# Hybrid decoder trunk on one core: the last output projection reads half of its weights already split, and the two row blocks are finished one after the other

## The chip, the cores and the metric

The kernel runs on 1 core of one Trainium2 chip. The metric is the device time of one execution in microseconds (us). Before the change the median of three runs is 2597.0 us (2596.93 to 2600.05). Engines are named as in the profile: PE is TensorE (matmul), PEld its weight load, DVE is VectorE, ACT is ScalarE, POOL is GpSimd, SP is SyncE, which here only issues DMA transfers. ACT and POOL also have a DMA queue each.

## The reference

Four layers; layer i has mixer i mod 3, so the last one (i = 3) is again multi-head latent attention. Everything is float32, with 256 rows of 2048.

```python
def reference(x, mem, norm_in, final_norm, mem_norm, rel_bias, w_in_a, ...):
    mem_n = _rmsnorm(mem, mem_norm)
    for i in range(DEPTH):
        h = _rmsnorm(x, norm_in[i])
        ...
            self_out, mq, gate = _mla_branch(h, w_in_a[j], ...)
        ...
        mem_out = _memory_attention(mq, mem_n @ w_mem_kv[i])
        y = jnp.concatenate([self_out, mem_out], axis=-1) * jax.nn.silu(gate)
        x = x + y @ w_out[i]
    return _rmsnorm(x, final_norm)

def _rmsnorm(x, g):
    xf = x.astype(jnp.float32)
    y = xf * lax.rsqrt(jnp.mean(xf * xf, axis=-1, keepdims=True) + EPS)
    return (y * g.astype(jnp.float32)).astype(x.dtype)
```

`y` has 3072 columns (2048 of the mixer, 1024 of the memory heads), so `w_out[i]` is 3072 x 2048. What the change touches is the last 512 rows of `w_out[3]`, the last residual addition, the final norm and the output.

## The kernel before

The 256 rows stand as two blocks `t` of 128 partitions; the running sum is `x[0]`, `x[1]` (128 x 2048 each, in SBUF for the whole run). A float32 product is made of three matmuls of float32r parts: each operand is split into a high part (`copy_act`, an ACT copy to float32r, line 60) and a low part (DVE subtraction, line 69), and the product is high x high + high x low + low x high.

Weights stream in through `stage` (line 205): one transfer on SP's queue of 512 KB, two blocks of 128 weight rows by 512 columns, into one of five `wr` buffers. `parts_of` (line 233) splits one block of 128 x 512 into `wh` and `wl` (three buffers each). `rows_by` (line 239) goes over the weight blocks `k` and multiplies each by both row blocks `t`: three matmuls of 512 columns for each `k` and `t` (lines 264 to 266), into two PSUM accumulators of the tag `acc` (four buffers). `columns_by` (line 269) is the same for products that come out transposed; the gates use it with the layer's normed input `nm.at`, four tiles of the tag `xT`.

The mixer's output comes in six parts `y` of 512 columns, in the order 4, 0, 1, 2, 3, 5 (line 984). Behind each part follows `w_out` (line 963) of the part before it: for each of four blocks `c` of 512 output columns a `rows_by` over the part's four weight blocks, then one addition into `x` for each row block (line 968). So the last call, `w_out` of part 5, stands alone at the end of the program.

In this last call each `c` is also squared and summed (line 978, ACT, into `f4`) and multiplied by the final norm's weights `fg` into `xg` (line 979, DVE). When all four are done, the sums of both row blocks are reduced, `rsqrt_mean` (line 151) works out the scale factors of both blocks with 12 small DVE instructions, and lines 1010 to 1018 scale and write four pieces of 128 x 1024: those of rows 0 to 127 by DVE and SP's queue, those of rows 128 to 255 by ACT and ACT's queue.

The order of instructions on each engine is worked out when the program is built, from dependences, buffers and assumed durations; an instruction may stand ahead of one that is written earlier. `tc.keep_in_program_order` ties an instruction behind the one written before it on its engine, and `tc.issue_after(i)` ties those of a block behind `i`; both set the order only. Side work is written as a generator in the list `steps`: `other_work` (line 228) advances the first one by two turns at each weight stage, which sets where its instructions are written.

`part_tile` gives one of two buffers of 128 x 512 (tag `hl`); only the grouped mixers of layers 1 and 2 use them. The tags `big0`, `big1` and `big2` hold the latent mixer's compressed vectors until its last projection, and then `xg` and `fg`.

Of the kernel before, what the change touches and what calls it, by code (L numbers as in the profile page):

```python
# [8 lines left out]
F32 = mybir.dt.float32  # L9
F32R = mybir.dt.float32r  # L10
I32 = mybir.dt.int32
AF = mybir.ActivationFunctionType
OP = mybir.AluOpType
AX = mybir.AxisListType

P = 128
S = 256
D = 2048
EPS = 1e-6
# [12 lines left out]
def kernel(ctx: ExitStack, tc: tile.TileContext, a: dict, out: bass.AP,  # L32
                             kinds=(0, 1, 2, 0)):
    nc = tc.nc
    depth = len(kinds)
    cst = ctx.enter_context(tc.tile_pool(name="cst", bufs=1))
    wp = ctx.enter_context(tc.tile_pool(name="wp", bufs=1))
    act = ctx.enter_context(tc.tile_pool(name="act", bufs=1))
    wk = ctx.enter_context(tc.tile_pool(name="wk", bufs=1))
    ps = ctx.enter_context(tc.tile_pool(name="ps", bufs=1, space=bass.MemoryType.PSUM))  # L40
    dr = ctx.enter_context(tc.tile_pool(name="dr", bufs=1, space=bass.MemoryType.DRAM))
# [4 lines left out]
    def tmp(name, n=512, dt=F32):  # L46
        return wk.tile([P, n], dt, name=name, tag=f"t{n}", bufs=3)

    def small(name, n, dt=F32, bufs=None):
        return wk.tile([P, n], dt, name=name, tag=f"s{n}" if bufs is None else name,  # L50
                       bufs=bufs or 6)

    def f32(ap):
        return ap.bitcast(F32)

    def part_tile(dt=F32R):
        return wk.tile([P, 512], dt, name="hl", tag="hl", bufs=2)

    def copy_act(o, i, scale=1.0):
        inst = nc.scalar.activation(o, i, AF.Copy, scale=scale)  # L60
        if pinned:
            tc.keep_in_program_order(inst)
# [9 lines left out]
    x = [cst.tile([P, D], F32, name=f"x{t}") for t in range(2)]  # L72
# [73 lines left out]
    def not_before(col):  # L146

        tc.keep_in_program_order(nc.gpsimd.tensor_copy(small("tick", 1), col))


    def rsqrt_mean(dst, ssq, n):
        m = ssq.shape[-1]
        v = small("rv", m)
        nc.vector.tensor_scalar(v, ssq, 1.0 / n, EPS, op0=OP.mult, op1=OP.add)
        i0 = small("ri", m, I32)
        nc.vector.tensor_scalar(i0, v.bitcast(I32), 1, None, op0=OP.arith_shift_right)
        i1 = small("rj", m, I32)
        nc.vector.tensor_scalar(i1, i0, -1.0, float(0x5F3759DF), op0=OP.mult, op1=OP.add)
        y = i1.bitcast(F32)
        for it in range(3):  # L160
            u = small("ru", m)
            nc.vector.scalar_tensor_tensor(u, y, -0.5, y, op0=OP.mult, op1=OP.mult)
            w = small("rw", m)
            nc.vector.tensor_mul(w, u, v)
            y2 = dst if it == 2 else small("ry", m)
            nc.vector.scalar_tensor_tensor(y2, w, 1.5, y, op0=OP.add, op1=OP.mult)
            y = y2
# [31 lines left out]

    def square_sum(col, src):  # L200
        junk = tmp("junk")
        nc.scalar.activation(junk[:, :src.shape[-1]], src, AF.Square, accum_out=col)


    def stage(w, k0, m, cols, each=None):
# [20 lines left out]
    steps = []  # L226

    def other_work():
        for _ in range(2):
            if steps and next(steps[0], None) is None:  # L230
                steps.pop(0)

    def parts_of(wr, c0, n):
        wh = wp.tile([P, 512], F32R, name="wh", tag="wh", bufs=3)
        wl = wp.tile([P, 512], F32R, name="wl", tag="wl", bufs=3)
        split(wh[:, :n], wl[:, :n], wr[:, c0:c0 + n])
        return wh, wl

    def rows_by(xt, kts, w, k0, cols, name, prepare=None, each=None, late=None):


        acc = [ps.tile([P, 512], F32, name=f"acc_{name}{t}", tag="acc", bufs=4) for t in range(2)]
        for s in range(0, kts, ST):
            m = min(ST, kts - s)
            wr, n = stage(w, k0 + s, m, cols, each)
            other_work()
            for k in range(m):
                if prepare is not None:
                    prepare(s + k)
                wh, wl = parts_of(wr, k * n, n)  # L250
                q = xt[(s + k) // 4]
                for t in range(2):
                    xh, xl = (q[:, v, (s + k) % 4, t * P:(t + 1) * P] for v in range(2))
                    first, last = s + k == 0, s + k == kts - 1
                    if late is not None and t == 0:

                        both = late[:, s + k].rearrange("p v c -> p (v c)")
                        if not last:
                            nc.tensor.matmul(acc[t][:, :n], both, wh[:, :n], start=first, stop=False)
                        nc.tensor.matmul(acc[t][:64, :n], both[:, :64], wl[:, :n], start=False, stop=False)  # L260
                        if last:
                            nc.tensor.matmul(acc[t][:, :n], both, wh[:, :n], start=False, stop=True)
                        continue
                    nc.tensor.matmul(acc[t][:, :n], xh, wh[:, :n], start=first, stop=False)  # L264
                    nc.tensor.matmul(acc[t][:, :n], xh, wl[:, :n], start=False, stop=False)  # L265
                    nc.tensor.matmul(acc[t][:, :n], xl, wh[:, :n], start=False, stop=last)  # L266
        return acc
# [682 lines left out]
            return y  # L950


    nm = Norm(0)
    memory()
    copies = [(v, g) for v in range(2) for g in range(4)]

    for i in range(depth):
        kind = kinds[i]
        mixer = Latent(nm, i, kinds[:i].count(0)) if kind == 0 else Grouped(nm, i, kind == 1)
        mixer.first()  # L960
        nxt = Norm(i + 1) if i + 1 < depth else None

        def w_out(part, y, last):
            for c in range(4):
                acc = rows_by([y], 4, a["w_out"][i], part * 4, (c * 512, 512), "wo")
                for t in range(2):
                    xs = x[t][:, c * 512:(c + 1) * 512]
                    nc.vector.tensor_add(xs, xs, acc[t])  # L968
                if c == 0 and copies:

                    not_before(xs[:, :1])
                    table_copies(*copies.pop(0))
                if last and nxt is not None:
                    nxt.chunk(c)
                if last and nxt is None:
                    for t in range(2):
                        xs = x[t][:, c * 512:(c + 1) * 512]
                        square_sum(f4[:, t * 4 + c:t * 4 + c + 1], xs)
                        nc.vector.tensor_mul(xg[t][:, c * 512:(c + 1) * 512], xs, fg[:, c * 512:(c + 1) * 512])

        if nxt is None:
            f4 = small("fs4", 8, bufs=1)
        pending = None
        order = [4, 0, 1, 2, 3, 5]
        for n_, part in enumerate(order):
            if part >= 4:
                y = memory_attend(*memory_project(nm, i, mixer.w, mixer.mq0, mixer.g0, part - 4,
                                                  f32(mixer.k[:, 0] if kind else mixer.kr)[:, 0, :1]))
            else:
                y = mixer.attend(*mixer.project(part))  # L990
            if pending is not None:
                w_out(*pending, False)
            pending = (part, y)
        if nxt is None:
            fg = act.tile([P, D], F32, name="fg", tag="big2")
            fn = a["final_norm"]
            nc.gpsimd.dma_start(fg, bass.AP(tensor=fn.tensor, offset=fn.offset, ap=[[0, P], [1, D]]))
            xg = [act.tile([P, D], F32, name="xg", tag=f"big{t}") for t in range(2)]
        w_out(*pending, True)
        if nxt is not None:  # L1000
            nxt.finish()
            nm = nxt


    ss = small("fss", 2)
    nc.vector.tensor_reduce(ss, f4.rearrange("p (t c) -> p t c", t=2), AX.X, OP.add)
    fr = small("fr", 2)
    rsqrt_mean(fr, ss, D)
    ov = out.rearrange("b (t p) d -> t p (b d)", p=P)
    for c in range(2):  # L1010
        for t in range(2):
            cs = slice(c * 1024, (c + 1) * 1024)
            if t == 0:
                nc.vector.tensor_scalar(xg[t][:, cs], xg[t][:, cs], fr[:, t:t + 1], None, op0=OP.mult)
                nc.sync.dma_start(ov[t][:, cs], xg[t][:, cs])
            else:
                copy_act(xg[t][:, cs], xg[t][:, cs], scale=fr[:, t:t + 1])
                nc.scalar.dma_start(ov[t][:, cs], xg[t][:, cs])


def _constants():
# [59 lines left out]
```

## Time and profile before

| | us |
|---|---|
| median of 3 runs | 2597.0 (2596.93 to 2600.05) |
| profiled execution | 2597.13 |
| its span, first to last instruction or landing of the program | 2595.3 |
| granted TensorE clock, mean | 0.998 |
| DMA traffic | 509.53 MB, 196 GB/s mean |

How to read the lines that follow. A group or timeline row has the line of the kernel, the engine, the operation and `out<-in` by tile names; in a timeline the first two numbers are start and duration in us, `xN` counts instructions merged into one row, and the bracket is the idle time of the engine just before, with what ended it. A row of the waits has who waited for what: us in total, times, longest. A row of a stretch `A:B` has its length, then the busy time of PE, PEld, DVE, ACT and POOL with the number of instructions, the granted clock, the busy share of the 16 DMA engines and GB/s. In the chain of waits, two neighbouring times differ by what the chain spent there, so a matmul counts with the time until the next one follows.

### The profile page before, as it was taken

Reading aid. Unit: us, or ns where it says so; the run is one execution under the profiler, and the core shown is the slowest. Engines: PE = TensorE matmul, PEld = TensorE weight load, DVE = VectorE, ACT = ScalarE, POOL = GpSimd, SP = SyncE. Lnnn points to the kernel's source line nnn. Section 1 sums busy time; section 2 is a strip of 40 time slices with the busy share of each in tenths; the row PEclk is TensorE's granted clock in tenths of the full one; section 3 lists DMA queues with packets and bytes.
Section 4 is the critical chain, followed back from the end, with each engine's and each line's share of the span. In section 5 each row is a group of like instructions: output and inputs, shape, how many; then the busy total and the mean of one; then the engine's idle time right before and its main releaser. Section 6 shows DMA issues by size and latency. Waiting matters only on the chain.

```text
span 2595.3 us, 41702 instructions
## 1 busy us (share of the span) xinstructions
PE 2576.4 (99%) x14066; PEld 2216.7 (85%) x14066; DVE 1880.5 (72%) x4130; ACT 1619.6 (62%) x3420; POOL 68.0 (3%) x124
## 2 busy tenths in 40 slices
PE   9999999999999999999999999999999999999997
PEld 7888898888888888888888888888888888888886
DVE  7666667667776686787778776777778767676667
ACT  6556556556656566667666666676666655665655
POOL 0100000000000010000000000000000000000000
PEclk9999999999999999999999999999999999999999
DMA  7888777666676667566556575555655766566664
GB/s 257 254 258 267 242 214 234 185 171 190 193 203 201 197 218 246 163 196 189 192 164 199 170 224 170 175 174 180 195 161 149 233 183 168 170 167 182 212 178 131
DMA packets 455128, 509.53 MB, mean 196 GB/s; under 512 B 68816, under 2 KB 351712, under 8 KB 453760
## 3 DMA queue, kind: packets, MB, share of 16 engines
q1 hardware_dynamic: 441392, 449.58, 57.9%
q0 software_dynamic: 13088, 56.16, 6.8%
q8 instruction: 110, 1.80, 0.3%
q10 hardware_dynamic: 432, 1.11, 0.1%
q14 instruction: 106, 0.87, 0.1%
HBM read 487.81 MB, written 31.56 MB: 200 GB/s over the span
## 4 chain that ended last, share of the span: by engine, by line
PE 99%; DVE 1%; ACT 0%; DMA 0%; SPq 0%; issue 0%; ACTq 0%
PE acc_g L284 14%; PE acc_g L288 7%; PE acc_wo L264 7%; PE acc_wo L265 7%; PE acc_wo L266 7%; PE acc_mk L284 5%; PE acc_mq L284 5%; PE acc_cq L284 3%; PE acc_qn L284 3%; PE acc_mq L288 2%; PE acc_mk L288 2%; PE acc_q L265 2%; PE acc_q L266 2%; PE acc_q L264 2%; PE acc_mv L265 2%; PE acc_mv L264 2%
## 5 line engine op out<-in xcount | busy, mean ns | idle before, releaser
L69 DVE TENSOR_TENSOR wl<-wr,wh 128x512 fp32r<-128x512 f32 (+2 forms) x1728 | 1165.0, 677 | 625.8 <-ACT wh L60 602.8
L60 ACT ACTIVATE wh<-wr 128x512 fp32r<-128x512 f32 (+2 forms) x1728 | 1070.4, 621 | 813.8 <-PE acc_g L284 179.3
L284 PE MATMUL acc_g<-xT,wh 128*128 128x512 f32 x1536 | 486.3, 396 | 0.0
L288 PEld LDWEIGHTS acc_g<-xT,wl 128*128 128x128 f32 x1536 | 284.8, 188 | 60.8
L288 PE MATMUL acc_g<-xT,wl 128*128 128x256 f32 x1536 | 310.5, 280 | 0.0
L265 PE MATMUL acc_wo<-wl,y 128*128 128x512 f32 x768 | 303.5, 395 | 0.2 <-DVE wl L69 0.2
L266 PE MATMUL acc_wo<-wh,y 128*128 128x512 f32 x768 | 298.2, 390 | 0.0
L284 PEld LDWEIGHTS acc_g<-xT,wh 128*128 128x128 f32 x1536 | 238.3, 189 | 4.4
L264 PE MATMUL acc_wo<-wh,y 128*128 128x512 f32 x768 | 240.1, 391 | 0.1
L265 PEld LDWEIGHTS acc_wo<-wl,y 128*128 128x128 f32 x768 | 144.3, 188 | 28.4 <-DVE wl L69 0.6
L266 PEld LDWEIGHTS acc_wo<-wh,y 128*128 128x128 f32 x768 | 144.3, 188 | 27.9
L264 PEld LDWEIGHTS acc_wo<-wh,y 128*128 128x128 f32 x768 | 142.2, 188 | 29.2 <-ACT y L60 1.0
L284 PE MATMUL acc_mk<-mT,wh 128*128 128x512 f32 x512 | 161.7, 396 | 0.3 <-DVE mv L418 0.3
L284 PE MATMUL acc_mq<-xT,wh 128*128 128x512 f32 x512 | 161.6, 396 | 0.0
L968 DVE TENSOR_TENSOR x<-x,acc_wo 128x512 f32<-128x512 f32 x192 | 126.1, 681 | 5.7 <-PE acc_wo L266 5.6
L284 PE MATMUL acc_qn<-cT,wh 128*128 128x512 f32 x384 | 121.2, 397 | 0.0
L284 PE MATMUL acc_cq<-xT,wh 128*128 128x512 f32 x384 | 120.8, 396 | 0.0
L288 PEld LDWEIGHTS acc_mk<-mT,wl 128*128 128x128 f32 x512 | 96.0, 188 | 22.3 <-DVE wl L69 0.4
L288 PEld LDWEIGHTS acc_mq<-xT,wl 128*128 128x128 f32 x512 | 94.0, 188 | 20.1
L288 PE MATMUL acc_mq<-xT,wl 128*128 128x256 f32 x512 | 103.3, 282 | 0.0
L288 PE MATMUL acc_mk<-mT,wl 128*128 128x256 f32 x512 | 101.9, 278 | 0.0
L265 PE MATMUL acc_q<-wl,xT 128*128 128x512 f32 x256 | 101.1, 395 | 0.0
(304 smaller groups left out, 4272.5 us busy)
## 6 DMA issues: line engine op xcount, KB each, us to landing
wr<-in_w_out_dram SPq DMA_DIRECT2D x192, 512.0 KB, 3.6
wr<-in_w_in_a_dram SPq DMA_DIRECT2D x176, 512.0 KB, 4.0
wr<-in_w_mem_kv_dram SPq DMA_DIRECT2D x120, 512.0 KB, 4.4
wr<-in_w_in_b_dram SPq DMA_DIRECT2D x112, 512.0 KB, 3.5
wr<-in_w_in_c_dram SPq DMA_DIRECT2D x104, 512.0 KB, 3.5
wr<-in_w_uq_dram SPq DMA_DIRECT2D x192, 128.0 KB, 2.5
wr<-in_w_uq_dram SPq DMA_DIRECT2D x48, 256.0 KB, 3.7
tab<-flat POOLq DMA_DIRECT2D x8, 1536.0 KB, 9.4
```

The source lines that it names most:

```text
L60: inst = nc.scalar.activation(o, i, AF.Copy, scale=scale)
L69: nc.vector.tensor_sub(lo, src, f32(hi))
L264: nc.tensor.matmul(acc[t][:, :n], xh, wh[:, :n], start=first, stop=False)
L265: nc.tensor.matmul(acc[t][:, :n], xh, wl[:, :n], start=False, stop=False)
L266: nc.tensor.matmul(acc[t][:, :n], xl, wh[:, :n], start=False, stop=last)
L284: nc.tensor.matmul(acc[j], wh[:, o:o + P], q[:, :, kt % 4, :], start=kt == 0, stop=False)
L288: nc.tensor.matmul(acc[j][:, 0, :], wl[:, o:o + P], q[:, 0, kt % 4, :], start=False, stop=kt == kts - 1)
L968: nc.vector.tensor_add(xs, xs, acc[t])
```

## The change

The last call of `w_out` is replaced by a function `last_out`.

- Columns 0 to 1023 are worked out as before, by `rows_by` with split weights.
- For columns 1024 to 2047 the split is done ahead of time: a generator `split_ahead`, added to `steps` in the last layer behind `mixer.first()`, loads eight blocks of 128 x 512 weights on POOL's queue, splits each (one ACT copy, one DVE subtraction, in the two `hl` buffers) and stores both parts to DRAM, four tiles `split_w` of 1 MB. `last_out` loads these into four tiles of the tag `xT`, again on POOL's queue.
- The products of these columns go by row block: both column blocks of rows 0 to 127 first, then columns 1024 to 1535 of rows 128 to 255, then the last 512 columns of these rows in two halves of 256. They are five accumulators and are tied in the order written.
- Sums of squares are formed by row block. `share` multiplies by -0.5/D and adds the sums of the earlier blocks; `rsqrt_of` starts from it with one instruction and makes three rounds of two (before: two and then three rounds of three, ahead of them a reduction and a scaling).
- Rows 0 to 127 are scaled and written in two pieces of 1024 columns, by DVE and SP's queue and by ACT and ACT's queue; rows 128 to 255 in four pieces of 640, 384, 640 and 384 columns, alternating between the two.
- The closing addition (last 256 columns of rows 128 to 255) is tied behind the last root instruction of rows 0 to 127.

```diff
     def square_sum(col, src):
         junk = tmp("junk")
-        nc.scalar.activation(junk[:, :src.shape[-1]], src, AF.Square, accum_out=col)
+        return nc.scalar.activation(junk[:, :src.shape[-1]], src, AF.Square, accum_out=col).ins
...
+    def last_out(w, part, y):
+        fg = act.tile([P, D], F32, name="fg", tag="big2")
...
+        xg = [act.tile([P, D], F32, name="xg", tag=f"big{t}") for t in range(2)]
+        f4 = small("fs4", 10, bufs=1)
...
+        def add(c0, n, t, acc, col):
+            xs = x[t][:, c0:c0 + n]
+            inst = nc.vector.tensor_add(xs, xs, acc)
+            return inst.ins, square_sum(f4[:, t * 5 + col:t * 5 + col + 1], xs)
+
+        def weigh(engine, c0, n, t):
+            cs = slice(c0, c0 + n)
+            engine.tensor_mul(xg[t][:, cs], x[t][:, cs], fg[:, cs])
+
+        def products(acc, t, k, wh, wl):
+            xh, xl = (y[:, v, k, t * P:(t + 1) * P] for v in range(2))
+            tc.keep_in_program_order(nc.tensor.matmul(acc, xh, wh, start=k == 0, stop=False))
+            tc.keep_in_program_order(nc.tensor.matmul(acc, xh, wl, start=False, stop=False))
+            tc.keep_in_program_order(nc.tensor.matmul(acc, xl, wh, start=False, stop=k == 3))
+
+        def share(dst, cols, rest):
+
+            if cols.shape[-1] > 1:
+                ss = small("fss", 1)
+                nc.vector.tensor_reduce(ss, cols, AX.X, OP.add)
+                cols = ss
+            nc.vector.tensor_scalar(dst, cols, -0.5 / D, rest, op0=OP.mult, op1=OP.add)
+
+        def rsqrt_of(v):
+
+            i1 = small("fj", 1, I32)
+            nc.vector.tensor_scalar(i1, v.bitcast(I32), -0.5, float(0x5F3759DF - (1 << 22) - (1 << 30)),
+                                    op0=OP.mult, op1=OP.add)
+            r = i1.bitcast(F32)
+            for it in range(3):
+                u = small("fu", 1)
+                nc.vector.scalar_tensor_tensor(u, r, v, r, op0=OP.mult, op1=OP.mult)
+                r2 = small("fy", 1)
+                inst = nc.vector.scalar_tensor_tensor(r2, u, 1.5, r, op0=OP.add, op1=OP.mult)
+                r = r2
+            return r, inst
+
+        def write(t, r, pieces):
+            for e, c0, c1 in pieces:
+                piece = xg[t][:, c0:c1]
+                if e == 0:
+                    nc.vector.tensor_scalar(piece, piece, r, None, op0=OP.mult)
+                    nc.sync.dma_start(ov[t][:, c0:c1], piece)
+                else:
+                    copy_act(piece, piece, scale=r)
+                    nc.scalar.dma_start(ov[t][:, c0:c1], piece)
+
+        early = [small(f"fe{t}", 1, bufs=1) for t in range(2)]
+        while steps:
+            other_work()
+        kept = []
+        for m in range(4):
+            q = act.tile([P, 2, 4, S], F32R, name="wk", tag="xT", bufs=4)[:].rearrange("p v k c -> p v (k c)")
+            nc.gpsimd.dma_start(q, split_w[m])
+            kept += [[q[:, v, k * 512:(k + 1) * 512] for v in range(2)] for k in range(2)]
+        for c in range(2):
+            acc = rows_by([y], 4, w, part * 4, (c * 512, 512), "wo")
+            for t in range(2):
+                add(c * 512, 512, t, acc[t], c)
+        acc = [ps.tile([P, 512], F32, name="acc_wo2", tag="acc", bufs=4) for c in range(5)]
+        for c in range(2):
+            for k in range(4):
+                products(acc[c], 0, k, *kept[c * 4 + k])
+        for k in range(4):
+            products(acc[2], 1, k, *kept[k])
+        for h in range(2):
+            for k in range(4):
+                products(acc[3 + h][:, :S], 1, k, *(w_[:, h * S:(h + 1) * S] for w_ in kept[4 + k]))
+        for t in range(2):
+            for c in range(2):
+                weigh(nc.vector, c * 512, 512, t)
+        for c in range(2):
+            add(1024 + c * 512, 512, 0, acc[c], 2 + c)
+            weigh(nc.vector, 1024 + c * 512, 512, 0)
+            if c == 0:
+                share(early[0], f4[:, :3], -0.5 * EPS)
+        v0 = small("fv", 1)
+        share(v0, f4[:, 3:4], early[0])
+        r, inst = rsqrt_of(v0)
+        write(0, r, ((0, 0, 1024), (1, 1024, 2048)))
+        add(1024, 512, 1, acc[2], 2)
+        share(early[1], f4[:, 5:8], -0.5 * EPS)
+        weigh(nc.vector, 1024, 512, 1)
+        add(1536, S, 1, acc[3][:, :S], 3)
+        weigh(nc.vector, 1536, S, 1)
+        v1, v2 = small("fv", 1), small("fv", 1)
+        share(v1, f4[:, 8:9], early[1])
+        with tc.issue_after(inst.ins):
+            add(1536 + S, S, 1, acc[4][:, :S], 4)
+        share(v2, f4[:, 9:10], v1)
+        weigh(nc.vector, 1536 + S, S, 1)
+        r, inst = rsqrt_of(v2)
+        write(1, r, ((0, 0, 640), (1, 1280, 1664), (0, 640, 1280), (1, 1664, 2048)))
+
+    split_w = [dr.tile([P, 2, 1024], F32R, name=f"sw{m}") for m in range(4)]
+
+    def split_ahead(w, part):
+        for n in range(8):
+            c, k = 2 + n // 4, n % 4
+            lo, hi = part_tile(), part_tile()
+            nc.gpsimd.dma_start(f32(lo), w[(part * 4 + k) * P:(part * 4 + k + 1) * P, c * 512:(c + 1) * 512])
+            for _ in range(6):
+                yield True
+            copy_act(hi, f32(lo))
+            nc.vector.tensor_sub(lo, f32(lo), f32(hi))
+            for v, p_ in enumerate((hi, lo)):
+                nc.gpsimd.dma_start(split_w[n // 2][:, v, n % 2 * 512:n % 2 * 512 + 512], p_)
+            for _ in range(6):
+                yield True
...
         mixer.first()
+        if i == depth - 1:
+            steps.append(split_ahead(a["w_out"][i], 5))
...
-                if last and nxt is None:
-                    for t in range(2):
-                        xs = x[t][:, c * 512:(c + 1) * 512]
-                        square_sum(f4[:, t * 4 + c:t * 4 + c + 1], xs)
-                        nc.vector.tensor_mul(xg[t][:, c * 512:(c + 1) * 512], xs, fg[:, c * 512:(c + 1) * 512])
...
         if nxt is None:
-            fg = act.tile([P, D], F32, name="fg", tag="big2")
-            fn = a["final_norm"]
-            nc.gpsimd.dma_start(fg, bass.AP(tensor=fn.tensor, offset=fn.offset, ap=[[0, P], [1, D]]))
-            xg = [act.tile([P, D], F32, name="xg", tag=f"big{t}") for t in range(2)]
-        w_out(*pending, True)
-        if nxt is not None:
+            last_out(a["w_out"][i], *pending)
+        else:
+            w_out(*pending, True)
             nxt.finish()
             nm = nxt
-
-    ss = small("fss", 2)
-    nc.vector.tensor_reduce(ss, f4.rearrange("p (t c) -> p t c", t=2), AX.X, OP.add)
-    fr = small("fr", 2)
-    rsqrt_mean(fr, ss, D)
-    ov = out.rearrange("b (t p) d -> t p (b d)", p=P)
-    for c in range(2):
-        for t in range(2):
-            cs = slice(c * 1024, (c + 1) * 1024)
-            if t == 0:
-                nc.vector.tensor_scalar(xg[t][:, cs], xg[t][:, cs], fr[:, t:t + 1], None, op0=OP.mult)
-                nc.sync.dma_start(ov[t][:, cs], xg[t][:, cs])
-            else:
-                copy_act(xg[t][:, cs], xg[t][:, cs], scale=fr[:, t:t + 1])
-                nc.scalar.dma_start(ov[t][:, cs], xg[t][:, cs])
```

More of the change, by code (lines that the diff above doesn't have):

```diff
@@ L950, in attend @@
             return y
+    def last_out(w, part, y):
+        fg = act.tile([P, D], F32, name="fg", tag="big2")
+        fn = a["final_norm"]
+        nc.gpsimd.dma_start(fg, bass.AP(tensor=fn.tensor, offset=fn.offset, ap=[[0, P], [1, D]]))
+        xg = [act.tile([P, D], F32, name="xg", tag=f"big{t}") for t in range(2)]
+        f4 = small("fs4", 10, bufs=1)
+        ov = out.rearrange("b (t p) d -> t p (b d)", p=P)
+        def add(c0, n, t, acc, col):
[83 more added lines that the diff above has]
+        write(1, r, ((0, 0, 640), (1, 1280, 1664), (0, 640, 1280), (1, 1664, 2048)))
@@ L974, in w_out @@
                     nxt.chunk(c)
-                if last and nxt is None:
-                    for t in range(2):
-                        xs = x[t][:, c * 512:(c + 1) * 512]
-                        square_sum(f4[:, t * 4 + c:t * 4 + c + 1], xs)
-                        nc.vector.tensor_mul(xg[t][:, c * 512:(c + 1) * 512], xs, fg[:, c * 512:(c + 1) * 512])
-        if nxt is None:
-            f4 = small("fs4", 8, bufs=1)
         pending = None
```

## The prediction

> **What bounds the kernel now.** I read the page's head and its chain of waits first, then the waits of TensorE alone, then the timeline of the last 15 us.
>
> ```profile
> span 2595.3 us, 41702 instructions
> PE 2576.4 (99%) x14066; PEld 2216.7 (85%) x14066; DVE 1880.5 (72%) x4130; ACT 1619.6 (62%) x3420; POOL 68.0 (3%) x124
> PE 99%; DVE 1%; ACT 0%; DMA 0%; SPq 0%; issue 0%; ACTq 0%
> PE spr L175 <- DVE dg L174: 2.6, 1, 2.6
> PE acc_wo L265 <- DVE wl L69: 0.2, 1, 0.2
> 2570.00:2580.00 10.00, 10.00 (x46) 8.29 (x45) 9.09 (x16) 6.44 (x15) 0.00 (x0) 1.00 0.00 1
> ```
>
> The chain is matmuls from one end to the other, and the waits of TensorE are a few single events: weights arrive in time. So there are two ways to gain: fewer matmul columns (the change keeps all of them), or a shorter stretch behind the last matmul. In the last row (us, busy of PE, PEld, DVE, ACT, POOL, then clock, DMA share, GB/s) VectorE works 9.09 of 10 us just ahead of the end. The tail, from the timeline:
>
> ```profile
> 2581.66 0.39 PE L266 MATMUL acc_wo<-wh,y 128*128 128x512 f32 x1
> 2581.63 1.29 DVE L968 TENSOR_TENSOR x<-x,acc_wo 128x512 f32<-128x512 f32 x2 [1.30 <-PE acc_wo L266]
> 2582.35 0.63 ACT L202 ACTIVATE junk<-x 128x512 f32<-128x512 f32 x1 [2.87 <-DVE x L968]
> 2582.89 0.19 ACT L202 ACTIVATION_READ_ACCUMULATOR junk<-x 128x1 f32 x1
> 2583.54 0.19 ACT L202 ACTIVATION_READ_ACCUMULATOR junk<-x 128x1 f32 x1
> 2584.03 0.15 DVE L1006 TENSOR_REDUCE fss<-fs 128x2 f32<-128x8 f32 x1
> 2586.39 0.16 DVE L166 SCALAR_TENSOR_TENSOR fr<-rw,ry 128x2 f32<-128x2 f32 x1
> 2586.59 2.19 ACT L60 ACTIVATE xg<-xg,fr 128x1024 f32<-128x1024 f32 x2 [2.86 <-DVE fr L166]
> 2586.59 1.42 DVE L1014 TENSOR_SCALAR xg<-xg,fr 128x1024 f32<-128x1024 f32 x2
> 2587.38 1.02 SPq L1015 DMA_DIRECT2D out_dram<-xg  x2
> 2588.00:2589.00 1.00, 0.00 (x0) 0.00 (x0) 0.01 (x1) 0.78 (x1) 0.00 (x0) 0.50 0.80 315
> 2589.00:2590.00 1.00, 0.00 (x0) 0.00 (x0) 0.00 (x0) 0.00 (x0) 0.00 (x0) 0.50 0.98 401
> 2592.00:2593.00 1.00, 0.00 (x0) 0.00 (x0) 0.00 (x0) 0.00 (x0) 0.00 (x0) 0.50 1.00 389
> 2593.00:2594.00 1.00, 0.00 (x0) 0.00 (x0) 0.00 (x0) 0.00 (x0) 0.00 (x0) 0.50 0.46 184
> ```
>
> From the first closing add at 2581.63 to the scale factor at 2586.59 are 4.96 us, from there to the end at 2595.3 are 8.71 us. In the second part the 2 MB of output are the larger item: the queue is full (share 1.00) at about 400 GB/s from 2588.2 to 2593.46, and 1.84 us follow the last byte. The profiled execution took 2597.13 us, so 1.83 us lie outside the span; it is 0.13 us above the median.
>
> **The change part by part.** Tail first, counted from the last matmul.
>
> *Matmuls.* The 48 products of columns 1024 to 2047 become 36 of 512 columns and 24 of 256.
>
> ```profile
> 2575.24 0.91 PE acc_wo L264 x4
> 2547.49 1.30 PE msp L575 x11
> 2547.33 1.46 PE L575 MATMUL msp<-mkr,mqT 128*128 128x256 f32 x11
> ```
>
> Four of 512 take 0.91 (0.2275 each), eleven of 256 take 1.30 (0.118 each; the last one is visible 0.16 later, 1.46 against 1.30). 48 x 0.2275 = 10.92; 36 x 0.2275 + 24 x 0.118 = 11.02: 0.10 longer. The old last product is issued by 2581.66 + 0.23 = 2581.89, the new one by 2581.99 and visible 0.16 later at 2582.15; with the 0.04 that the old add waits behind its product, the closing add starts at 2582.2, 0.57 later than now.
>
> *Closing chain.* Only 256 columns of one row block are left, where now 2 x 512 are.
>
> ```profile
> L295 DVE TENSOR_TENSOR z<-z,acc_g x4: 411/413/414, 2523.2 to 2535.9; 128x256 f32<-128x256 f32 x4
> 2026.53 0.40 ACT L656 ACTIVATE cqs<-z 128x256 f32<-128x256 f32 x1
> ```
>
> Add 0.41, hand-over 0.04, square 0.40, its sum read out by 0.10 behind the square (2582.89 + 0.19 against 2582.35 + 0.63), hand-over to VectorE 0.30 (2583.73 to 2584.03): 2583.45. Then one sum step and seven steps of the root, 8 small instructions at (2586.59 - 2584.03) / 13 = 0.197 each, where 13 were: 2585.03. The scale factor comes 1.56 earlier. The fifth accumulator reuses the first one's bank, whose add is 8 us old by then.
>
> *VectorE's backlog.* The factor of rows 0 to 127 is now worked out during the last products. From 2571.2, when columns 0 to 1023 are summed, VectorE has 2 adds and some 2 weighings left over, then add and weighing of three blocks of 512 (0.68 each, as the old adds above: 1.29 for two), add and weighing of 256 (0.41 + 0.37), 6 sum and 7 root steps at 0.197, and a scaling of 1024 at 1.42 / 2 = 0.71: 1.3 + 1.4 + 4.1 + 0.8 + 2.5 + 0.7 = 10.8 us into 11.0. But it must idle where a product isn't ready: about 1.4 us while the second accumulator fills. So when the last product is ready it is between 0 and 1.3 us behind, and the order of its queue says how much of that stands ahead of the closing add. The closing add is also tied behind the last root step of rows 0 to 127, and the second factor, its scalings and its four transfers wait for that add. I take about the middle, +0.6, and keep both ends.
>
> *Scaling and writing.* First piece of 640 columns 0.71 x 640 / 1024 = 0.44; from the end of a first piece (2586.59 + 0.71) to the first bytes 0.9 as now; 1.05 MB at 400 GB/s 2.62; 1.84 behind them: 5.80 against 8.71, so -2.91. The other pieces are scaled within 1.0 us, before the queue runs dry. Rows 0 to 127 must be out of the way: their factor is due between 2580.1 and 2581.4, so their megabyte flows until 2586 at the latest, and the next begins at 2585.63 + 0.44 + 0.9 = 2587.0.
>
> [...]
>
> *The splits brought forward.* Eight ACT copies (0.63) and eight subtractions (0.69) move out of the last 10 us; their number stays. What covers them is idle time of ACT and VectorE (38% and 28% by the page). New are 8 loads and 16 stores of 256 KB and 4 loads of 1 MB on POOL's queue, which is empty for 401 us of the last layer; SP's queue loses four weight loads of 512 KB:
>
> ```profile
> 2423.86 0.53 POOL L997 DMA_DIRECT2D fg<-in_final_norm_dram  x1 [401.61 <-PE acc_qn L288]
> 109.38 0.63 ACT L202 ACTIVATE junk<-x 128x512 f32<-128x512 f32 x1 [1.05 <-DMA x<-in_x_dram]
> DMA to landing us min/median/max: 4.8/5.4/6.2
> ACT junk L202 <- DMA x<-in_x_dram: 1.6, 2, 1.1
> 2033.85 0.63 ACT L60 ACTIVATE wh<-wr 128x512 fp32r<-128x512 f32 x1 [0.76 <-PE acc_cq L284]
> 2035.24 0.63 ACT L60 ACTIVATE wh<-wr 128x512 fp32r<-128x512 f32 x1 [0.76 <-PE acc_cq L284]
> DMA to landing us min/median/max: 3.1/5.2/6.1
> bm<-tab POOLq DMA_DIRECT2D x8, 1024.0 KB, 6.4
> L288 PE MATMUL acc_g<-xT,wl x64: 274/278/287, 2511.2 to 2533.0; 128*128 128x256 f32 x64
> 2000.00:2050.00 50.00, 50.00 (x318) 45.35 (x317) 34.91 (x84) 34.56 (x78) 2.32 (x5) 1.00 0.82 248
> ```
>
> The load of the final norm stands last in the program and yet ran as soon as its buffer was free: instructions go into the queues when they are expected ready, not where they are written. So the six turns that the splitter yields don't hold its copies back; each copy will stand in ACT's queue where its 256 KB load is expected. Behind a copy that waits stand the splits of the weights, and TensorE waits for those. The one like case is the squares of x behind 256 KB loads (landing 4.8 to 6.2, third row): 2 of 8 held ACT, by 1.05 us at most, and TensorE noticed nothing. Its cover: three split buffers, one in use; two stages of 1.39 (2035.24 - 2033.85) less copy and subtraction leave 2 x 1.39 - 0.63 - 0.69 = 1.4 us. 1.05 is under 1.4, so I price the splits at 0; the other end is a wait by a whole store landing, 3.1 to 6.1 (the 512 KB stores of the memory values, row "3.1/5.2/6.1"), less 1.4, eight times: 14 to 38 us.
>
> *The kept parts come back.* Their buffers are those of the layer's input, last read at 2533.0 + 0.28. Four loads of 1 MB at 6.4, even one behind the other, are in at 2559; the first is used at 2571.0, so 12 us of cover. If they crowd the weight loads: the row of 2000 to 2050 has four POOL loads of 512 KB within 2 us, 248 GB/s, and TensorE busy 50.00 of 50. Price 0.
>
> The sum: 2597.13 - 1.56 + 0.6 - 2.91 = 2593.3, which is 3.7 us or 0.14% below the median of 2597.0. With the two ends of the backlog it is 2592.7 to 2594.0.
>
> **The rivals.**
>
> *ACT held by the splitter's loads (slower).* Place: the eight copies; for it speaks that nothing pins them, and that the store before each load must land too, on the same two buffers; against it the 1.05 us above. It decides from a hold of 1.4 + 3.9 / 8 = 1.9 us each, where the 3.9 us gained in the tail are gone, and is slower by 0.2% from 1.4 + 9 / 8 = 2.5 us. Priced at the shortest store landing, 3.1 - 1.4 = 1.7 each: 2593.3 + 13.6 = 2606.9.
>
> *The kept parts late (slower).* The fourth load is needed at 2571.0 + 18 x 0.2275 = 2575.1, so loads one behind the other decide from (2575.1 - 2533.3) / 4 = 10.4 us each, 1.6 times the 6.4 seen. At twice 10.4 TensorE would wait 42 us: 2635.
> The Trainium skill speaks for this one (SBUF — State Buffer, two separate sides): a POOL-issued transfer can't get its descriptors written while VectorE holds the port pair they share. In this trace the same kind of load took 6.4 us with VectorE 72% busy.
>
> *Both megabytes leave together.* If VectorE's order puts the root of rows 0 to 127 behind the adds of the others, 2 MB flow at the end as now, and 2.62 comes back: 2595.9. For it: 10.8 us of work in 11.0; against: rows 0 to 127 have 5.5 us of lead.
>
> *More than the sum.* No backlog (-0.6), and the 0.9 ahead of the first byte and 1.84 behind the last, seen for a burst of 2 MB, halved for one of 1 MB (-1.37): 2591.3. For it: landings grew from 2.7 to 5.5 us as the queue filled:
>
> ```profile
> DMA to landing us min/median/max: 2.7/4.3/5.5
> ```
>
> **How the numbers follow.** Sum as reckoned 0.55 (2592.4 to 2594.4); both together 0.12 (2595.9); more than the sum 0.17 (2591.3); ACT held 0.13 (2606.9); kept parts late 0.03 (2635). What a measurement of this kernel tells from no change is about 0.2%, 5.2 us: 2591.8 to 2602.2. Faster by more is the fourth case, 0.17; slower the two with stalls, 0.16; within it 0.67. The range runs from 2591.0, just under the fourth case, to 2599.0, which takes in holds of 2.1 us on each copy; outside are the dearer holds, the late parts and a rest below, under 0.2.
>
> **What would show it.** Right: the scale factor of the second block some 3 us after the last matmul, two separate bursts of about 2.6 us at 400 GB/s, the first over before the second; no wait of TensorE for "acc_wo2"; end of span 3 to 4.5 us earlier. Wrong: ACT idle in front of its copy into "hl" by more than 1.4 us with a gap in TensorE behind it; the first "acc_wo2" product behind a DMA of "wk"; the closing add more than 1.3 us behind its product; one burst of 5 us.

## The result and the profile after

The changed kernel takes 2610.18 us (median of 6 runs, 2608.8 to 2612.54), the kernel before 2598.45 us (6 runs, 2596.93 to 2600.05); the ratio is 1.0046, 95% interval 1.0035 to 1.0056. It is slower by 0.46%, outside the predicted range, and the span of the profiled execution grew from 2595.3 to 2607.8 us.

The page of the changed kernel, in its head, its busy tenths and its chain:

```profile
span 2607.8 us, 41801 instructions
PE   9999999999999999999999999999989999999998
PE 96%; DMA 2%; issue 1%; ACT 1%; DVE 1%; POOL 0%; SPq 0%; POOLq 0%; ACTq 0%; DVEq 0%
```

Two things are new. One slice of PE, the 30th of 40, has an 8 (there was none before), and 2% of the chain of waits is now DMA. The slices are 65 us long, so the place is near 1900 us, in layer 2, one layer ahead of the one that the change is about. The rows of two stretches, first of the changed kernel, then of the kernel before (length, then busy time of PE, PEld, DVE, ACT, POOL with the number of instructions, clock, DMA share, GB/s):

```profile
1800.00:1845.00 45.00, 45.00 (x237) 38.05 (x236) 31.81 (x84) 29.42 (x74) 0.00 (x0) 1.00 0.53 163
1845.00:1935.00 90.00, 82.43 (x437) 67.49 (x436) 62.73 (x152) 55.56 (x132) 14.92 (x27) 0.98 0.76 233
```

```profile
1800.00:1845.00 45.00, 45.00 (x238) 38.03 (x237) 32.49 (x88) 28.99 (x74) 0.21 (x1) 1.00 0.53 164
1845.00:1935.00 90.00, 90.00 (x514) 77.82 (x513) 70.26 (x175) 62.39 (x152) 1.78 (x3) 1.00 0.60 188
```

In the same 90 us TensorE issues 437 matmuls where it issued 514. VectorE and ACT have *less* to do there too, so it isn't that these engines are full. The timeline of POOL and of ACT in the changed kernel shows what happens:

```profile
1855.83 0.55 POOL L1062 DMA_DIRECT2D hl<-in_w_out_dram  x1 [8.55 <-PE tr L465]
1880.34 0.53 POOL L1068 DMA_DIRECT2D sw<-hl  x1 [4.45 <-ACT e L60]
1881.06 0.53 POOL L1068 DMA_DIRECT2D sw<-hl  x1 [0.19 <-issue]
1886.31 0.55 POOL L1062 DMA_DIRECT2D hl<-in_w_out_dram  x1 [4.71 <-DMA sw<-hl]
...
1930.84 0.53 POOL L1068 DMA_DIRECT2D sw<-hl  x1 [0.20 <-DVE sa L537]
```

```profile
1860.85 0.63 ACT L60 ACTIVATE hl<-hl 128x512 fp32r<-128x512 f32 x1 [0.24 <-DMA hl<-in_w_out_dram]
...
1871.29 0.63 ACT L60 ACTIVATE hl<-hl 128x512 fp32r<-128x512 f32 x1 [3.61 <-DMA hl<-in_w_out_dram]
...
1885.10 0.63 ACT L60 ACTIVATE wh<-wr 128x512 fp32r<-128x512 f32 x1 [0.76 <-PE acc_mq L284]
1891.02 0.63 ACT L60 ACTIVATE hl<-hl 128x512 fp32r<-128x512 f32 x1 [5.29 <-DMA hl<-in_w_out_dram]
1891.56 0.61 ACT L60 ACTIVATE wh<-wr 128x512 fp32r<-128x512 f32 x1
...
1929.19 0.63 ACT L60 ACTIVATE hl<-hl 128x512 fp32r<-128x512 f32 x1 [2.07 <-issue]
```

All eight turns of the splitter run between 1855 and 1931 us, as soon as the `hl` buffers are free of layer 2's last use (`PE tr`). Each ACT copy of `hl` finds its load not landed; for two of the eight the profile names no releaser, but they start 7.0 and 4.6 us after their loads were issued, and the eight loads took 4.0 to 6.9 us to land. Follow one turn: the stores at 1880.34 and 1881.06 must land before the next load may overwrite the buffer, so that load goes out at 1886.31; ACT has been standing before the copy since 1885.73 and gets to it at 1891.02. Behind the copy in ACT's queue stands the next weight split, which TensorE needs. The eight brackets add up to 22.5 us, the longest 5.29. In seven of the eight turns ACT's idle time begins only after the load was issued, in the turn just followed 0.58 us before it. So ACT stands while the load itself is on its way, and the store's landing acts by sending the load out late. What TensorE then waits for are `wh` of ACT and `wl` of VectorE (the first two rows have no counterpart in the list of before, the third stood there with 0.2 us):

```profile
PE acc_g L284 <- ACT wh L60: 2.5, 2, 2.2
PE acc_mq L284 <- ACT wh L60: 1.7, 2, 1.3
PE acc_wo L265 <- DVE wl L69: 1.6, 3, 0.9
```

The list shows only part of the loss, since a matmul counts as busy beyond the time at which the next follows (at the end of the kernel before, one of 512 columns is shown 0.39 us long while the next starts after 0.23). So I take landmarks, instructions that both kernels have: the last table load of layer 2 and the small copy that POOL makes when the last layer's `kr` is ready. Before, they stand 175.10 apart:

```profile
1844.79 0.88 POOL L898 DMA_DIRECT2D bm<-tab  x1 [76.55 <-DVE mn L517]
2019.89 0.19 POOL L148 COPY tick<-kr 128x1 f32<-128x1 f32 x1 [173.11 <-ACT kr L60]
```

In the changed kernel, with the last product:

```profile
1845.83 0.88 POOL L898 DMA_DIRECT2D bm<-tab  x1 [76.55 <-DVE mn L517]
2036.06 0.19 POOL L148 COPY tick<-kr 128x1 f32<-128x1 f32 x1 [104.69 <-ACT kr L60]
2598.16 0.28 PE L974 MATMUL acc_wo<-wk,y 128*128 128x256 f32 x1
```

They are 190.23 apart: 15.13 us lost. From there to the issue of the last product (its start plus 0.23 for 512 columns, 0.12 for 256) it is 2598.28 - 2036.06 = 562.22 against 2581.89 - 2019.89 = 562.00. The rest is the tail, here with the scaling of rows 0 to 127 on VectorE, the closing add, the second factor, and the queue:

```profile
2597.87 0.75 DVE L1002 TENSOR_SCALAR xg<-xg,fy 128x1024 f32<-128x1024 f32 x1
2598.59 0.41 DVE L963 TENSOR_TENSOR x<-x,acc_wo 128x256 f32<-128x256 f32 x1
2601.22 0.16 DVE L994 SCALAR_TENSOR_TENSOR fy<-fu,fy 128x1 f32<-128x1 f32 x1
2601.42 1.01 DVE L1002 TENSOR_SCALAR xg<-xg,fy 128x640 f32<-128x640 f32 x2
2601.00:2602.00 1.00, 0.00 (x0) 0.00 (x0) 0.93 (x4) 0.58 (x2) 0.00 (x0) 0.50 1.01 401
2602.00:2603.00 1.00, 0.00 (x0) 0.00 (x0) 0.43 (x1) 0.54 (x2) 0.00 (x0) 0.50 0.22 85
2603.00:2604.00 1.00, 0.00 (x0) 0.00 (x0) 0.00 (x0) 0.00 (x0) 0.00 (x0) 0.50 0.99 378
2605.00:2606.00 1.00, 0.00 (x0) 0.00 (x0) 0.00 (x0) 0.00 (x0) 0.00 (x0) 0.50 0.65 230
```

The queue is full until 2602, empty for most of a microsecond and full again until 2605.65: the two megabytes leave one after the other. From the last product's issue to the end of the span it is 2607.8 - 2598.28 = 9.5 us, against 2595.3 - 2581.89 = 13.4. The balance: 1.04 more up to the first landmark, where the two programs do the same, 15.13 in the middle, 0.22, and -3.9 in the tail make 12.5, the whole difference of the spans.

### The profile page after: what moved, and what is told of

Read it like the earlier page. It is cut to its first block, busy times and chain, and to the rows that moved or that the text cites. A ratio compares the mean times of both kernels' runs of the same rounds, so it can differ in the third digit from the quotient of the medians.

```text
span 2607.8 us, 41801 instructions
## 1 busy us (share of the span) xinstructions
PE 2584.3 (99%) x14078; PEld 2219.9 (85%) x14078; DVE 1880.9 (72%) x4141; ACT 1618.2 (62%) x3423; POOL 83.0 (3%) x152
## 2 busy tenths in 40 slices
DMA packets 457849, 517.92 MB, mean 199 GB/s; under 512 B 69233, under 2 KB 352385, under 8 KB 455969
## 4 chain that ended last, share of the span: by engine, by line
PE 96%; DMA 2%; issue 1%; ACT 1%; DVE 1%; POOL 0%; SPq 0%; POOLq 0%; ACTq 0%; DVEq 0%
PE acc_g L284 13%; PE acc_g L288 7%; PE acc_wo L264 6%; PE acc_wo L265 6%; PE acc_wo L266 6%; PE acc_mk L284 5%; PE acc_mq L284 4%; PE acc_cq L284 3%; PE acc_qn L284 3%; PE acc_mk L288 2%; PE acc_q L265 2%; PE acc_q L266 2%; PE acc_q L264 2%; PE acc_mv L265 2%; PE acc_mv L264 2%; PE acc_mv L266 2%
## 5 line engine op out<-in xcount | busy, mean ns | idle before, releaser
L265 PE MATMUL acc_wo<-wl,y 128*128 128x512 f32 x752 | 297.3, 395 | 1.6 <-DVE wl L69 1.6
L266 PE MATMUL acc_wo<-wh,y 128*128 128x512 f32 x752 | 291.6, 390 | 0.0
L264 PE MATMUL acc_wo<-wh,y 128*128 128x512 f32 x752 | 235.8, 392 | 1.9 <-ACT wh L60 1.4
L264 PEld LDWEIGHTS acc_wo<-wh,y 128*128 128x128 f32 x752 | 139.2, 188 | 31.3 <-ACT wh L60 2.6
L266 PEld LDWEIGHTS acc_wo<-wh,y 128*128 128x128 f32 x752 | 141.3, 188 | 27.2
L1090 DVE TENSOR_TENSOR x<-x,acc_wo 128x512 f32<-128x512 f32 x184 | 120.7, 681 | 3.6 <-PE acc_wo L266 3.5
```

## The experiments

Three theories stood against each other: ACT held by the splitter's copies, the additional traffic itself, and the new tail. The first four runs were made on one chip, with a median of 2598.92 us for the kernel before, the last three on another, where it took 2597.50 us (one run).

**The copies tied to their place.**

```diff
-            copy_act(hi, f32(lo))
+            tc.keep_in_program_order(nc.scalar.activation(hi, f32(lo), AF.Copy))
             nc.vector.tensor_sub(lo, f32(lo), f32(hi))
```

> The eight ACT copies of the splitter are tied behind the ACT instruction written before them; all else is the changed kernel. Held-ACT theory (the copies stood in ACT's queue where their loads were not in yet, about 22 us of holds in all, 15 us of them passed on to TensorE between 1845 and 2020 us): the holds shrink to under 1.4 us each, TensorE loses no more than 3 us there, and the time is 2595 us (2593 to 2598), 0.1% under the kernel before. Traffic theory (12 MB more on the queues and POOL's descriptors slow the weights themselves, wherever the copies stand): 2607 to 2611 us. Tail theory (the new order of the last products costs the time): 2609 us or more.

2595.88 us (11 runs, 2593.95 to 2597.81), ratio 0.9991, interval 0.9982 to 0.9999. The view of the `hl` tile between 1840 and 2300 us has the copies in the last layer and none of them waiting for a load; the landmarks are back where they were:

```profile
L1062 POOL DMA_DIRECT2D hl<-in_w_out_dram x8: 549/549/552, 1856.4 to 2201.9; - x8
L1065 ACT ACTIVATE hl<-hl x8: 614/617/617, 2087.6 to 2213.7; 128x512 fp32r<-128x512 f32 x8
L1068 POOL DMA_DIRECT2D sw<-hl x16: 534/534/544, 2088.5 to 2215.4; - x16
```

```profile
1846.37 0.88 POOL L898 DMA_DIRECT2D bm<-tab  x1 [76.54 <-DVE mn L517]
2021.47 0.19 POOL L148 COPY tick<-kr 128x1 f32<-128x1 f32 x1 [164.02 <-ACT kr L60]
```

2021.47 - 1846.37 = 175.10, to the hundredth the value of before. The same eight loads, sixteen stores and four loads are made: both pages have 517.92 MB, 8.4 MB more than before (10.5 on POOL's queue, 2.0 less on SP's; the 12 of the expectation was too many). So the traffic theory falls, and with the changed tail in place the tail theory falls too. That the traffic hurt only at its old place is answered by the changed kernel's list of waits between 1845 and 2040 us: no engine waits there for a load into `wr`, so the weights were in time. Where the splits run now, TensorE is busy without a gap while POOL's transfers raise the traffic (0.66 and 176 GB/s in the same stretch before):

```profile
2100.00:2220.00 120.00, 120.00 (x667) 103.87 (x666) 87.71 (x180) 73.57 (x146) 10.78 (x20) 1.00 0.80 220
```

**The tail alone.**

```diff
-            nc.gpsimd.dma_start(q, split_w[m])
+            wr, n = stage(w, part * 4 + m % 2 * 2, 2, ((2 + m // 2) * 512, 512))
+            for k in range(2):
+                split(q[:, 0, k * 512:(k + 1) * 512], q[:, 1, k * 512:(k + 1) * 512], wr[:, k * 512:(k + 1) * 512])
...
-        if i == depth - 1:
-            steps.append(split_ahead(a["w_out"][i], 5))
```

> No splitter and no trip through DRAM: the last four weight loads come on SP's queue as before, ACT and VectorE split them straight into the four kept tiles once these are free; the tail is that of the changed kernel. Held-ACT theory and traffic theory: 2594.5 us (2593 to 2597), since the tail alone is 3.9 us shorter in the trace (9.5 us against 13.4 behind the last product); if VectorE, which is 8 to 9 tenths busy there, falls behind, up to 3 us more. Tail theory: 2609 us or more.

2598.47 us (11 runs), ratio 0.9998, interval 0.9990 to 1.0007: no change, above the main expectation and inside the allowance for VectorE. Its trace shows where the gain went. The tail is 9.5 us long, as in the changed kernel. But from the `kr` landmark to the last product it is 564.90 us in place of 562.00: splitting late costs 2.9 us of TensorE, in stretches where it had been busy throughout.

```profile
2540.00:2560.00 20.00, 19.63 (x98) 15.70 (x96) 17.35 (x34) 14.40 (x32) 0.00 (x0) 1.00 0.67 204
2560.00:2588.00 28.00, 27.08 (x136) 22.17 (x134) 22.21 (x46) 13.26 (x31) 0.00 (x0) 1.00 0.13 43
```

VectorE is at 17.35 of 20 us in the first of them (15.59 before). But ACT is held here too: its copies into the kept tiles stand in its queue before their weight loads have landed, three times between 2547 and 2556 us, and the longest wait of TensorE that follows is for ACT:

```profile
ACT wk L60 <- DMA wr<-in_w_out_dram: 3.9, 3, 2.1
2561.15 0.73 PE L264 MATMUL acc_wo<-wh,y 128*128 128x512 f32 x2 [0.85 <-ACT wh L60]
```

How much of the 2.9 us is VectorE's load and how much ACT's holds, no run separates. In this run the splits of the kept tiles, made late, cost what the tail gains: the tail's gain is real, but it goes back into TensorE's gaps.

**The splitter alone**, in the kernel before, with its parts never read:

```diff
         mixer.first()
+        if i == depth - 1:
+            steps.append(split_ahead(a["w_out"][i], 5))
...
+        while nxt is None and steps:
+            other_work()
         w_out(*pending, True)
```

> The kernel before with the splitter added, whose parts are stored and never read back; end of the program as before. Held-ACT theory: 2613 us (2610 to 2617), 15 us above the kernel before, with ACT held about 22 us at the eight copies. Traffic theory: also slower, but without long holds of ACT. Tail theory: 2598.5 us, no change.

2615.21 us (4 runs), ratio 1.0065, interval 1.0050 to 1.0080. The landmarks are 190.51 apart, 15.4 more than before, with the tail at its old 13.4 us. ACT is held 19.6 us at the eight copies, a little less than expected; most of it has the splitter's loads as releaser:

```profile
ACT hl L60 <- DMA hl<-in_w_out_dram: 17.0, 5, 4.6
POOL hl L959 <- DMA sw<-hl: 11.5, 5, 5.0
```

**Thirty turns in place of six.**

```diff
-            for _ in range(6):
+            for _ in range(30):
```

> The splitter yields 30 turns in place of 6 before and after each copy, so its instructions are written over five times as much of the last layer. Held-ACT theory, with the order set by when things are expected ready: the copies stay between 1855 and 1935 us, ACT is held some 20 us, 2608 to 2613 us. If the turns do set the place, the copies spread over the last layer, the holds go, and the time is 2595 us.

2611.89 us (one run; 2598.92 for the kernel before). The landmarks are 189.01 apart and ACT is held 21.2 us in all. The copies stay where they were, so the turns are not what sets their place:

```profile
L60 ACT ACTIVATE hl<-hl x8: 618/632/633, 1863.8 to 1931.3; 128x512 fp32r<-128x512 f32 x8
```

**Without the later stores.**

```diff
-            nc.gpsimd.dma_start(q, split_w[m])
+            nc.gpsimd.dma_start(q, split_w[0])
...
             for v, p_ in enumerate((hi, lo)):
-                nc.gpsimd.dma_start(split_w[n // 2][:, v, n % 2 * 512:n % 2 * 512 + 512], p_)
+                if n < 2:
+                    nc.gpsimd.dma_start(split_w[0][:, v, n % 2 * 512:n % 2 * 512 + 512], p_)
```

> The changed kernel with the copies untied, in which only the first two weight blocks are stored to DRAM and all four kept tiles are read from these, so the output is made with wrong weights for columns 1024 to 2047; the eight loads and splits stay. Now a load waits for the subtraction of the turn before, and no longer for a store to land. If both legs of the round trip are late: the holds of ACT sink from 22.5 us to 8 us or less (about 1 us each, as the squares of x behind loads of the same size), the copies follow each other at 8 us in place of 9.8, and the last product comes 12 to 15 us earlier than in the changed kernel. If the load alone is late: the holds stay at 17 us or more.

2597.12 us (one run; 2597.50 for the kernel before). The wait rows of this kernel:

```profile
ACT hl L60 <- DMA hl<-in_w_out_dram: 8.3, 5, 3.0
POOL hl L1062 <- DVE hl L1066: 27.0, 5, 5.7
```

ACT is held 8.3 us in all, a little over the 8 that were expected, the longest time by 3.0 on the second copy, ahead of which a store still stands; the others are at most 2.06. The copies follow each other at 6.8 us (8 were expected). The landmarks are 177.27 apart, 2.2 us over the kernel before in place of 15.1, and the last product is issued at 2585.78, 12.5 us earlier than in the changed kernel. So the load leg alone, which I had measured by the squares of `x`, costs little; most of the loss needs the store ahead of it, which sends the load out late. The run takes traffic away as well, but the first experiment has all of the traffic and no loss. With the stores gone the order of ACT's instructions may also have been made otherwise; that isn't separated here.

**The tail taken apart.** Two runs on the version with tied copies (9.7 us from the last product to the end). The first has the old root's 12 instructions:

```diff
-            i1 = small("fj", 1, I32)
-            nc.vector.tensor_scalar(i1, v.bitcast(I32), -0.5, float(0x5F3759DF - (1 << 22) - (1 << 30)),
-                                    op0=OP.mult, op1=OP.add)
+            w0 = small("fw", 1)
+            nc.vector.tensor_scalar(w0, v, -2.0, None, op0=OP.mult)
+            i0 = small("fi", 1, I32)
+            nc.vector.tensor_scalar(i0, w0.bitcast(I32), 1, None, op0=OP.arith_shift_right)
+            i1 = small("fj", 1, I32)
+            nc.vector.tensor_scalar(i1, i0, -1.0, float(0x5F3759DF), op0=OP.mult, op1=OP.add)
...
+                w1 = small("fw", 1)
+                nc.vector.tensor_mul(w1, u, w0)
...
```

> The version with the copies tied, with the root of the kernel before (12 small instructions in place of 7, for both row blocks; one more in front restores the mean). From the last product to the end of the span 9.7 us become 10.7 to 11.0 (five or six more instructions at 0.2), if the root's instructions are worth their number; unchanged, if the output queue sets the end.

2599.49 us (one run). The last product is issued at 2586.60 (0.12 after its start), the span ends at 2597.7: 11.1 us, 1.4 more, a little above what was expected, and not for the reason given. The second root itself takes 2.31 us (2589.01 to 2591.32) in place of 1.53: its five instructions more are worth 0.8 us. The closing add, which is tied behind the first block's longer root, starts 0.3 us behind its product (started at 2586.48, 0.28 long, so ready at 2586.76), where the version with the short root has 0.15. The scaling of rows 0 to 127 now stands behind that add and not ahead of it, and the last sum step follows the add's start by 1.70 us in place of 1.24.

```profile
2587.07 0.41 DVE L963 TENSOR_TENSOR x<-x,acc_wo 128x256 f32<-128x256 f32 x1
2587.40 0.74 DVE L1007 TENSOR_SCALAR xg<-xg,fy 128x1024 f32<-128x1024 f32 x1
```

The second writes rows 0 to 127 only after the other block's root:

```diff
-        write(0, r, ((0, 0, 1024), (1, 1024, 2048)))
+        r0 = r
...
         r, inst = rsqrt_of(v2)
+        hold = small("fh", 1)
+        nc.vector.scalar_tensor_tensor(hold, r, 0.0, r0, op0=OP.mult, op1=OP.add)
+        write(0, hold, ((0, 0, 1024), (1, 1024, 2048)))
         write(1, r, ((0, 0, 640), (1, 1280, 1664), (0, 640, 1280), (1, 1664, 2048)))
```

> The version with the copies tied, in which rows 0 to 127 are scaled and written only after the root of rows 128 to 255, so that both megabytes leave together. If the early write is worth its transfer: from the last product to the end of the span 9.7 us become 12.3 to 13.0 (1.05 MB at 400 GB/s and one small instruction). If the transfer isn't what sets the end: under 11.

2601.37 us (one run), of which 3.6 lie outside the span, where the kernel before has 1.8; so the spans are compared. 2597.8 - 2585.66 = 12.1 us, 2.4 more, a little under what was expected: the second factor comes 0.26 us earlier here (3.19 after the start of the last product, 3.45 with the early write), and the early megabyte is worth about its time in the queue. Added up, the two edits give back 3.8 us, about all that the tail of this version had gained (13.4 - 9.7 = 3.7); a run with both was not made.

## Why the prediction was wrong, point by point

- **Matmuls** (+0.10, the last product at another width): right; the stretch up to the last product's issue is 0.22 longer, including every other change in the last layer. The bank of the fifth accumulator had been free for 6.0 us when its first product came (add at 2590.17, 0.69 long; product at 2596.84), not 8, and nothing waited for it.
- **Closing chain** (factor 2.88 us after the last product is ready): right, 2601.42 - 2598.44 = 2.98.
- **VectorE's backlog** (0 to 1.3, taken as +0.6): mis-sized, 0.15 in place of 0.6. The closing add starts 0.15 us after its product is ready, behind the scaling of rows 0 to 127 (2597.87 + 0.75 above). Adds and weighings had slipped between the root steps of rows 0 to 127 (lines 992 and 994; line 963 is the add of columns 1024 to 1535 of rows 128 to 255), so little was left over:

```profile
2595.39 0.22 DVE L992 SCALAR_TENSOR_TENSOR fu<-fy,fv 128x1 f32<-128x1 f32 x1
2595.61 0.69 DVE L963 TENSOR_TENSOR x<-x,acc_wo 128x512 f32<-128x512 f32 x1
2596.21 0.15 DVE L994 SCALAR_TENSOR_TENSOR fy<-fu,fy 128x1 f32<-128x1 f32 x1
```

- **Scaling and writing** (5.80): mis-sized the other way, 2607.8 - 2601.42 = 6.4. Of the 0.22 in the microsecond from 2602, 0.08 is the end of the first megabyte; the second starts at 2602.86. It took until 2605.65, 2.8 in place of 2.62, its first bytes came 1.44 after the factor in place of 1.34, and 2.15 follow the last in place of 1.84. The two errors cancel: the tail was to give 3.9 and gives 3.9, to the tenth by luck.
- **The kept parts** (price 0): right. They were issued from 2541.4 to 2549.7 and landed within 10.1 us, slower than the 6.4 of the prediction but some 27 us before the first was used at 2587.2.

```profile
L1014 POOL DMA_DIRECT2D wk<-sw x4: 528/528/528, 2541.4 to 2549.7; - x4
DMA to landing us min/median/max: 6.9/9.2/10.1
```

- **The splits brought forward** is the step that failed: "1.05 is under 1.4, so I price the splits at 0". That the copies would run when expected ready and not where they are written was right, and thirty turns confirm it. The like case was not alike: the squares of `x` stand behind one load that waits for nothing. Here each load but the first waits for a store, on two buffers, so two landings come between one copy and the next: the store's sends the load out late, and ACT stands before the copy for what is left of the load's. I had named the store for the rival and then priced the main case by the other leg alone. In place of 0 TensorE lost 15.1 us in the changed kernel, inside the other end that I had reckoned (14 to 38 us from a whole store landing): it lost 15.4 with the splitter alone, 2.2 where the later stores are gone, 0.00 with the copies tied. The cover was about right: 1.4 us off each of the six brackets above it leaves 13.2 of the 22.5 us. A copy that idles ACT by more than 1.4 us with gaps of TensorE behind it was also the first of the signs that I had named for being wrong.
- **The rival that came true** is ACT held, priced at 2606.9 with a chance of 0.13; it lies 3.3 us under the measured 2610.18. Its price took the shortest store landing eight times, 13.6. That this comes near the 15.13 is in part luck, since the holds run from 0.24 to 5.29 us and two of them are under the cover. It also started from the time of one execution, 2597.13, where the median of the six runs is 2598.45; the programs' starts differ by some microseconds from run to run (below). What was wrong is the reason for so low a chance: a case with half the mechanism.

Open stays what landing was assumed when the order was made; only its result, the order and the holds, is shown. Whether loads on SP's queue would come earlier wasn't tried, nor more `hl` buffers.

## What to carry to other kernels

A side stream of load, work, store on few buffers is paced by two landings per turn, and its work instruction, put into a busy engine's in-order queue where the schedule expects the data, holds all that stands behind it; here, tying it behind the work among which it was meant to run took the whole loss away. Before pricing it by a like case, count the landings between two uses of a buffer in both. When a gain at one end of a program is on the order of microseconds, set landmarks along the trace, since a loss one layer away can outweigh it while the changed part does exactly what was reckoned.

## What the runs showed of the hardware

Up to the first landmark the order of the instructions on each engine is the same in all nine kernels, and yet it stands at 1844.79 us in the kernel before, 1845.83 in the changed one and up to 1849.31 in the others: 4.5 us of scatter over nine profiled executions that has nothing to do with the edits. From there on, stretches without holds agree to 0.05 us (175.10 before and with tied copies, 175.11 with the tail alone, 175.09 with the long root, 175.06 with the joint write). The distances say more than the medians when the effect is 2 or 3 us.

The tie also gives the fastest of these kernels: 0.9991 of the kernel before (0.9982 to 0.9999), 14.3 us under the changed kernel's median.
